# A bidirectional RWKV-7 scan inside a hybrid encoder layer: 32-token blocks laid out by direction and half of the heads, with v's products added in PSUM

## The chip, the cores and the metric

The kernel runs on one core of one Trainium2 chip. A core has a matrix engine (TensorE, in the profile PE for matmuls and PEld for weight loads), a vector engine (VectorE, DVE), a scalar engine (ScalarE, ACT), a general engine (GpSimd, POOL) and a sync engine (SP) whose queue issues most of the DMAs. Each engine takes its instructions in order and waits on semaphores of the others. Matmuls read SBUF and write PSUM, which has eight banks of 512 fp32 columns on 128 partitions; DVE and ACT carry results from PSUM back to SBUF. The metric is the device time of one execution in microseconds (us).

## The reference

The program is one encoder layer for 2048 tokens of width 1024: a normalisation, one wide projection, an RWKV-7 branch that is scanned forwards and backwards, a dilated attention branch, a merge and a mixture of experts. The change touches only the RWKV-7 scan. There are 8 heads of 64 channels, and for each head and direction a state S of 64 x 64:

```python
def step(S, inp):
    r_t, w_t, k_t, v_t, a_t, b_t = inp
    sa = jnp.einsum('bhij,bhj->bhi', S, a_t)
    S = S * w_t[:, :, None, :] + sa[..., None] * b_t[:, :, None, :] + v_t[..., None] * k_t[:, :, None, :]
    return S, jnp.einsum('bhij,bhj->bhi', S, r_t)
...
for d, reverse in enumerate((False, True)):
    ...
    wkv = wkv + wkv7_scan(rh, heads(decay), kd, vh, -kk, kk * ah, reverse)
```

## The kernel before

The scan is done in chunks of 32 tokens (`CH`), 64 steps in all. Step j takes chunk j for the forward direction (d = 0) and chunk 63 - j for the backward one (d = 1), for all 8 heads at once. Inside a chunk the recurrence becomes small matrix products. With A (from the normalised keys) and R (from r) stacked in `ar`, B and K stacked in `bk`, and their transposes in `bt`:

- Z = A S + (A K) v is the right-hand side, 32 x 64 for each head and direction.
- U = inverse x Z, where the inverse is of the triangular 32 x 32 matrix made from A B.
- S' = S + B' U + K' v, after which S is scaled with the chunk's decay `WC`.
- Y = R S + (R B) U + (R K) v is the output, written to `y_d`.

Three kinds of work surround the steps. `prep(i, hh)` prepares 128 tokens (four chunks) for four of the heads: gates by small matmuls (line 431), exponentials, `bk` and `ar` (lines 469 to 474), PE transposes into `bt` (line 479), and the products `bk` x `ar`, masked into `M` (lines 488 and 490). `invert(jj)` inverts the triangular matrices of 256 tokens: DVE transposes them from `M` into `X` (line 513), DVE and POOL eliminate column by column, and DVE transposes back (line 534). `add_v(i, d)` (lines 406 and 412) adds the product of A K and v into the same tile that holds v, ahead of the steps. `dense()` is the other large part: it multiplies the hidden state with the attention and gate columns of the projection, as matmuls of 256 or 512 columns (lines 686 and 690), from weights that come by DMA (line 628) and are split in two parts by ACT and DVE (lines 630 and 631).

The text of the program sets how these are woven: `fill(n)` puts n units of `dense()` (six matmuls of 256 columns or three of 512) behind each part. A step calls it three times through `between` (3.1 units each), `prep` and `invert` at each of their `yield`s. A scheduler then settles the order on each engine, close to that of the text. PE's order is fixed from there on: where a matmul waits, all behind it wait.

In the layout before, a block of 32 tokens of one chunk lies on 32 partitions and all 8 heads lie along the free dimension. Chunks of even number have partitions 0 to 63, those of odd number 64 to 127, and the two directions of a step always have different parity. In the tile `uv` the first 32 partitions of a half take U (and before it the product of A K and v), the other 32 hold v; so one matmul over 64 partitions multiplies U and v together (lines 583 and 591). The matmuls of a step thus use 64 x 64, 64 x 32 (K x M) or 32 x 32 places of the array. U is written back in pieces by DVE (line 574) and ACT (line 576). PSUM banks: `pre` two, `ZY` two, `Up` one, `Sp` one, and two for `dense`.

```python
for ds_, d, c4, b, qc, M in info:
    PE.matmul(ZY[b:b + 64, o], AR[i, h // 4][ds_, h % 4, c4], St[ds_, h], start=h == 0, stop=False, ...)
...
PE.matmul(Up[d][b + h % 2 * 32:b + h % 2 * 32 + 32, h // 2], M[b:b + 32, qc, h, 0:CH], Zs[b:b + 32, o], ...)
```

Of the kernel before, what the change touches and what calls it, by code (L numbers as in the profile page):

```python
# [23 lines left out]
H = 8  # L24
# [18 lines left out]
def hybrid_layer_kernel(ctx, tc, x, positions, norm1_g, w_in, mu_prev, mu_next, w_decay0, w_decay_up, a_gate0,  # L43
# [289 lines left out]

    NC = T // CH
# [16 lines left out]
    nc.sync.dma_start(upw[64:128], a_gate_up[0].rearrange("d p c -> p d c"))  # L351
    msk = mk(sc, [128, 2, 64], F32, "msk")
# [7 lines left out]
    for p in range(1, 4):  # L360
        V.tensor_copy(msk[p * 32:(p + 1) * 32], msk[0:32])
# [21 lines left out]
    AR, BT, UV = {}, {}, {}  # L383
    MR = [mk(sc, [128, 3, 2, H, 64], F32, f"M{d}") for d in range(2)]
    rkk = rkk_d.rearrange("(w a) (e n) t -> n w a e t", w=3, e=2)
    fl = "p a b -> p (a b)"

    def load_v(i):


        uv = UV[i] = mk(sc, [128, 4, HD], F32, "uv", bufs=2)
        vc = v_d.rearrange("(c s) f -> c s f", s=CH)
        for j in range(4 * i, 4 * i + 4):
            for d, c in enumerate((j, NC - 1 - j)):
                p = c % 2 * 64
                nc.sync.dma_start(uv[p + 32:p + 64, j % 4], vc[c])

    def add_v(i, d):

        uv, M = UV[i], MR[d][:, i % 3]  # L400
        pa = mk(psA, [128, 2, H // 2, N], F32, "pre", bufs=2)
        for s in range(4):
            c = s if d == 0 else 3 - s
            for h in range(H):
                p, o = c % 2 * 64, c % 2 * 64 + h % 2 * 32
                PE.matmul(pa[o:o + 32, s // 2, h // 2], M[p + 32:p + 64, c // 2, h, 0:CH],
                          uv[p + 32:p + 64, s, h * N:(h + 1) * N], start=True, stop=True)
        for p in range(2):
            s = p if d == 0 else 1 - p
            for e in range(2):  # L410
                o = p * 64 + e * 32
                S.activation(uv[p * 64:p * 64 + 32, s::2].rearrange("p s (h e n) -> p s h e n", e=2, n=N)[:, :, :, e],
                             pa[o:o + 32], AF.Copy)

    def prep(i, hh):

        ti = (i, NT - 1 - i)
        tk = [slice(t * 128, (t + 1) * 128) for t in ti]
        ld = mk(wk, [128, 3, 4, 128], F32, "ld", bufs=1)
        for d in range(2):  # L420
            for w in range(3):
                nc.sync.dma_start(ld[d * 64:(d + 1) * 64, w].rearrange("n (a e) t -> n a e t", e=2),
                                  rkk[:, w, 2 * hh:2 * hh + 2, :, tk[d]])
        r, k, kk = (ld[:, w] for w in range(3))
        t = [mk(wk, [128, 4, 128], F32, f"t{m}") for m in range(2)]
        for m in range(2):
            z = mk(psA, [128, 4, 128], F32, "pre", bufs=2)
            for h4 in range(4):
                h = hh * 4 + h4
                for d in range(2):  # L430
                    PE.matmul(z[d * 64:(d + 1) * 64, h4], upw[m * 64:(m + 1) * 64, d, h * 64:(h + 1) * 64],
                              sx[m * 64:(m + 1) * 64, tk[d]], start=True, stop=True)
            for h4 in range(4):
                o = 8 * m + hh * 4 + h4
                S.activation(t[m][:, h4], z[:, h4], AF.Tanh, scale=0.5, bias=Q[:, o:o + 1])
            yield
# [11 lines left out]
        hs = slice(hh * 4, hh * 4 + 4)  # L448
        S.activation(WC[0:64, 4 * i:4 * i + 4, hs].rearrange("p c h -> p h c"), cs[0:64, :, CH - 1::CH], AF.Exp)
        for c in range(4):  # L450

            j = 4 * i + 2 - c
            if j >= 0:
                S.activation(WC[64:128, j, hs], cs[64:128, :, c * CH + CH - 1], AF.Exp, scale=-1.0)
        yield
        kf = mk(wk, [128, 4, 128], F32, "cs")
        for h4 in range(4):
            h = hh * 4 + h4
            S.activation(kf[:, h4], ta[:, h4], AF.Identity, scale=Q[:, 24 + h:25 + h], bias=Q[:, 16 + h:17 + h])
# [3 lines left out]
        bt = BT[i, hh] = mk(sc, [128, 2, 4, 128], F32, "bt", bufs=6)  # L463
        bk = mk(wk, [128, 4, 4, 64], F32, "bk")
# [11 lines left out]
        for cp in range(2):  # L476
            pt = mk(psA, [128, 4, 128], F32, "pre", bufs=2)
            for h4 in range(4):
                PE.transpose(pt[:, h4], bk[:, h4, 2 * cp:2 * cp + 2].rearrange("p c x -> p (c x)"), ident)
            S.activation(bt[:, cp], pt, AF.Copy)  # L480
        for d in range(2):
            yield
            pm = mk(psA, [128, 2, 4, 64], F32, "pre", bufs=2)
            for cp in range(2):
                for h4 in range(4):
                    for p in range(2):
                        c = 2 * cp + p
                        PE.matmul(pm[p * 64:(p + 1) * 64, cp, h4], bk[d * 64:(d + 1) * 64, h4, c],
                                  ar[d * 64:(d + 1) * 64, h4, c], start=True, stop=True)
            V.tensor_tensor(MR[d][:, i % 3, :, hs], pm, msk[:, d, None, None, :].to_broadcast([128, 2, 4, 64]),  # L490
                            op=OP.mult)
        yield
        pb = mk(psA, [128, 4, 128], F32, "pre", bufs=2)
        for h4 in range(4):
            PE.matmul(pb[h4 * 32:(h4 + 1) * 32, 0], rkb[:, hh * 4 + h4], kf[:, h4], start=True, stop=True)
        bs = mk(wk, [128, 128], F32, "bs")
        S.activation(bs, pb[:, 0], AF.Copy)
        for d in range(2):
            nc.sync.dma_start(bon_d[d, hs, tk[d]], bs[d:128:32])

    def invert(jj):
# [4 lines left out]
        for d in range(2):  # L506
            M = MR[d][:, lo:hi + 1:hi - lo].rearrange("p i c h x -> p i (c h) x")
            for p in range(2):
                g = (2 * d + p) * 32
                src = M[p * 64:p * 64 + 32, :, :, 0:CH].rearrange("p i q t -> p t i q")  # L510
                xv = X[g:g + 32] if d == 1 else X[g:g + 32].rearrange("p x y -> p y x")
                xv = xv.rearrange("p t (i q) -> p t i q", i=2)
                V.transpose(xv, src)
                views.append((src, xv))
# [24 lines left out]
    def step(j, between):  # L539
        nonlocal St  # L540
        last = j == NC - 1
        i = j // 4
        if j:
            V.tensor_tensor(St, St, WC[:, j - 1, :, None].to_broadcast([128, H, 64]), op=OP.mult)
        ZY = mk(psA, [128, 512], F32, "ZY", bufs=2)
        cc = (j, NC - 1 - j)
        info = []
        for d, c in enumerate(cc):
            info.append((slice(d * 64, d * 64 + 64), d, c % 4, (c % 2) * 64, c // 2 % 2, MR[d][:, i % 3]))
        uv = UV[i][:, j % 4]  # L550
        for h in range(H if j else 0):
            o = slice(h * 64, h * 64 + 64)
            for ds_, d, c4, b, qc, M in info:
                PE.matmul(ZY[b:b + 64, o], AR[i, h // 4][ds_, h % 4, c4], St[ds_, h], start=h == 0, stop=False,
                          skip_group_check=True)
        Zs = mk(wk, [128, 512], F32, "Zs")
        if j:
            V.tensor_tensor(Zs, ZY, uv, op=OP.add)
        else:
            V.tensor_copy(Zs, uv)  # L560
        between(0)


        Up = [mk(psA, [128, H // 2, 64], F32, t) for t in ("Up", "Sp")]
        for h in range(H):
            o = slice(h * 64, h * 64 + 64)
            for ds_, d, c4, b, qc, M in info:
                PE.matmul(Up[d][b + h % 2 * 32:b + h % 2 * 32 + 32, h // 2], M[b:b + 32, qc, h, 0:CH], Zs[b:b + 32, o],
                          start=True, stop=True)
        for ds_, d, c4, b, qc, M in info:  # L570
            uh = uv[b:b + 32].rearrange("p (h e n) -> p h e n", e=2, n=N)
            for e in range(2):
                if d == 0:
                    V.tensor_copy(uh[:, :, e], Up[d][b + e * 32:b + e * 32 + 32])
                else:
                    S.activation(uh[:, :, e], Up[d][b + e * 32:b + e * 32 + 32], AF.Copy)
        between(1)
        if not last:
            Sp = mk(psA, [128, H, 64], F32, "Sp")
            for h in range(H):  # L580
                o = slice(h * 64, h * 64 + 64)
                for ds_, d, c4, b, qc, M in info:
                    PE.matmul(Sp[ds_, h], BT[i, h // 4][b:b + 64, qc, h % 4, ds_], uv[b:b + 64, o], start=True,
                              stop=True)
            Sn = mk(sc, [128, H, 64], F32, "St", bufs=2)
            V.tensor_tensor(Sn, Sp, St, op=OP.add)
            St = Sn
        for h in range(H):
            o = slice(h * 64, h * 64 + 64)
            for ds_, d, c4, b, qc, M in info:  # L590
# [3 lines left out]
        if j:  # L594
            S.activation(Ys, ZY, AF.Copy)
        for ds_, d, c4, b, *_ in info:
            if j == 0:
                S.activation(Ys[b + 32:b + 64], ZY[b + 32:b + 64], AF.Copy)
# [945 lines left out]
```

## Time and profile before

| | |
|---|---|
| runs, median of 3 | 3421.84 us (3415.53 to 3463.06) |
| profiled execution, its own time | 3408.95 us |
| its span, first to last instruction | 3407.2 us |
| PE busy in the span | 3131.7 us (92%) |
| DVE busy | 2340.0 us (69%) |
| ACT busy | 1630.8 us (48%) |
| POOL busy | 607.2 us (18%) |
| stretch of the scan | 424 to 1856 us |

A row of the timeline gives the start, the length, engine, line, operation, the tile written and those read, the shapes and the count of merged instructions, and in square brackets the idle time before it and what ended it. A row by line gives total busy time and the mean of one in ns after the first bar, and the engine's idle time ahead of the group after the second. A row of waits gives the total in us, how often, and the longest. A row by stretch gives its length, then for each engine the busy time and the count of instructions, the granted clock of TensorE as a share of full speed, the busy share of the DMA engines and GB/s. Matmuls overlap, so a group's busy time is less than its count times its mean, and each matmul in fp32 appears as two records of a matmul and two of a weight load.

### The profile page before, as it was taken

Reading aid. Unit: us, or ns where it says so; the run is one execution under the profiler, and the core shown is the slowest. Engines: PE = TensorE matmul, PEld = TensorE weight load, DVE = VectorE, ACT = ScalarE, POOL = GpSimd, SP = SyncE. Lnnn points to the kernel's source line nnn. Section 1 sums busy time; section 2 is a strip of 40 time slices with the busy share of each in tenths; the row PEclk is TensorE's granted clock in tenths of the full one; section 3 lists DMA queues with packets and bytes.
Section 4 is the critical chain, followed back from the end, with each engine's and each line's share of the span. In section 5 each row is a group of like instructions: output and inputs, shape, how many; then the busy total and the mean of one; then the engine's idle time right before and its main releaser. Section 6 shows DMA issues by size and latency. Waiting matters only on the chain. (4 is left out here: it accounts for less than half of the span.)

```text
span 3407.2 us, 72671 instructions
## 1 busy us (share of the span) xinstructions
PE 3131.7 (92%) x29105; PEld 2544.4 (75%) x29105; DVE 2340.0 (69%) x4364; ACT 1630.8 (48%) x3129; POOL 607.2 (18%) x728
## 2 busy tenths in 40 slices
PE   6999989999998989898989998989886999999997
PEld 4888778778876888688867886777775666777775
DVE  7243268677968787769674665667765677888885
ACT  5333344645464535463534765112122566777764
POOL 1000012121212021202020000433422311122231
PEclk8999989999999999998999999999998999999999
DMA  8234233443334323343334554434332799999996
GB/s 303 75 126 144 77 118 108 121 148 115 98 117 147 114 88 115 115 134 97 107 102 137 180 158 150 131 121 140 116 110 103 265 309 305 337 338 338 335 315 208
DMA packets 375953, 567.73 MB, mean 167 GB/s; under 512 B 32462, under 2 KB 232726, under 8 KB 370876
## 3 DMA queue, kind: packets, MB, share of 16 engines
q1 hardware_dynamic: 351100, 497.89, 44.3%
q0 software_dynamic: 13408, 53.10, 5.6%
q10 hardware_dynamic: 11104, 12.06, 1.2%
q8 instruction: 230, 3.77, 0.5%
q14 instruction: 111, 0.91, 0.1%
HBM read 444.05 MB, written 121.64 MB: 166 GB/s over the span
## 5 line engine op out<-in xcount | busy, mean ns | idle before, releaser
L686 PE MATMUL dn<-wh,hk 128*128 128x256 f32 x3456 | 478.0, 297 | 26.2 <-DVE wh L631 17.7
L1237 DVE TENSOR_TENSOR wh<-raw,wh 128x1024 fp32r<-128x1024 f32 x376 | 442.6, 1222 | 77.8 <-ACT wh L1236 77.2
L686 PEld LDWEIGHTS dn<-wh,hk 128*128 128x128 f32 x3456 | 447.4, 201 | 44.6 <-DVE wh L631 20.0
L1236 ACT ACTIVATE wh<-raw 128x1024 fp32r<-128x1024 f32 x384 | 386.9, 1053 | 144.6 <-DMA raw<-in_w_down_dram 60.8
L690 PE MATMUL dn<-hk,wh 128*128 128x512 f32 x1536 | 397.2, 406 | 26.0 <-DVE wh L631 17.0
L1366 PE MATMUL pgu<-wh,xT 128*128 128x512 f32 x1536 | 374.7, 400 | 2.1 <-ACT xT L1341 2.1
L690 PEld LDWEIGHTS dn<-hk,wh 128*128 128x128 f32 x1536 | 281.8, 191 | 101.0 <-DVE wh L631 23.8
L1366 PEld LDWEIGHTS pgu<-wh,xT 128*128 128x128 f32 x1536 | 285.5, 189 | 79.0 <-issue 7.3
L631 DVE TENSOR_TENSOR wh<-raw,wh 128x512 fp32r<-128x512 f32 x272 | 204.1, 754 | 132.7 <-ACT wh L630 131.5
L630 ACT ACTIVATE wh<-raw 128x512 fp32r<-128x512 f32 x272 | 170.7, 631 | 216.1 <-DMA raw<-in_w_in_dram 154.4
L280 PE MATMUL pp<-hq,wh 128*128 128x512 f32 x1008 | 253.8, 409 | 0.0
L280 PEld LDWEIGHTS pp<-hq,wh 128*128 128x128 f32 x1008 | 195.0, 195 | 46.5 <-ACT hq L217 0.4
L1122 PE MATMUL px<-wO,mT 128*128 128x512 f32 x768 | 207.7, 417 | 8.5 <-ACT mT L1112 5.9
L471 POOL TENSOR_TENSOR t<-t,ld 128x512 f32<-128x512 f32 x32 | 52.8, 1651 | 878.6 <-DVE t L460 612.7
L1410 PE MATMUL py<-wh,hT 128*128 128x512 f32 x768 | 191.4, 401 | 0.4 <-ACT hT L1388 0.4
L1122 PEld LDWEIGHTS px<-wO,mT 128*128 128x128 f32 x768 | 145.2, 197 | 46.2 <-ACT mT L1112 8.3
L1410 PEld LDWEIGHTS py<-wh,hT 128*128 128x128 f32 x768 | 140.5, 188 | 33.0 <-issue 1.2
L1302 POOL DMA_INDIRECT out_dram<-ys,IDX x49 | 91.0, 1857 | 315.1 <-issue 107.2
L283 ACT ACTIVATE u<-pp 128x512 f32<-128x512 f32 x56 | 61.2, 1093 | 161.1 <-PE pp L280 123.6
L1106 PE MATMUL ab<-yT,wA 128*128 128x256 f32 x768 | 118.1, 298 | 16.2 <-DVE tg L1108 12.8
L1326 POOL DMA_INDIRECT xg<-h_d,IDX x49 | 74.4, 1518 | 276.1 <-PE tx L1340 173.2
L1106 PEld LDWEIGHTS ab<-yT,wA 128*128 128x128 f32 x768 | 100.0, 192 | 30.6 <-DVE tg L1108 21.1
(421 smaller groups left out, 5770.9 us busy)
## 6 DMA issues: line engine op xcount, KB each, us to landing
raw<-in_w_in_dram SPq DMA_DIRECT2D x286, 256.0 KB
raw<-in_w_gate_dram SPq DMA_DIRECT2D x64, 1024.0 KB
raw<-in_w_up_dram SPq DMA_DIRECT2D x64, 1024.0 KB
raw<-in_w_down_dram SPq DMA_DIRECT2D x64, 1024.0 KB
ld<-rkk_d SPq DMA_DIRECT2D x192, 128.0 KB
g_d<-gs SPq DMA_DIRECT2D x64, 256.0 KB
tg<-g_d SPq DMA_DIRECT2D x128, 128.0 KB
qkr<-qkv_d SPq DMA_DIRECT2D x62, 256.0 KB
```

The source lines that it names most:

```text
L280: PE.matmul(pp, whs[k // 4][:, a, k % 4], hq[q][k // 2][:, k % 2, b], start=n == 0, stop=n == 3 * KT - 1)
L630: S.activation(wh[:, 0], raw, AF.Copy)
L631: V.tensor_tensor(wh[:, 1], raw, wh[:, 0], op=OP.subtract)
L686: PE.matmul(pp[e][:, j * 256:(j + 1) * 256], lhs(2 * e + j, hk, k, a), wk_[:, b], start=k + j + m == 0, stop=k + j + m == KT + 2, skip_gro ...
L690: PE.matmul(pp[e], wk_[:, a, e * 128:e * 128 + 128], hk[k // 2][:, k % 2, b], start=k + m == 0, stop=k + m == KT + 1)
L1106: PE.matmul(pa, wt[k][:, a, cs_], src[:, k, b], start=n == 0, stop=n == 3 * nk - 1)
L1122: PE.matmul(px, mT[:, k, a], wO[k][:, b, fs], start=n == 0, stop=n == 3 * KT - 1)
L1236: S.activation(wh[:, 0, ks], raw[:, ks], AF.Copy)
L1237: eng.tensor_tensor(wh[:, 1, ks], raw[:, ks], wh[:, 0, ks], op=OP.subtract)
L1302: G.indirect_dma_start(out=x2_d, out_offset=bass.IndirectOffsetOnAxis(ap=idx, axis=0), in_=src, in_offset=None, bounds_check=T - 1, oob_is ...
L1366: PE.matmul(pgu[n], xT[:, x_, 4 * a + k], wh[:, w_, k], start=a + k + m == 0, stop=a + k + m == 6)
L1410: PE.matmul(py[f], hT[:, x_, 2 * a + k], wh[:, w_, k, f * 512:(f + 1) * 512], start=a + k + m == 0, stop=a + k + m == 4)
```

## The change

A block is now 32 tokens of one direction d and one half e of the heads: it lies on partitions 64 d + 32 e, and four heads lie along the free dimension. All four blocks of a step (two directions, two halves) fill the 128 partitions whatever the chunk's number. `MB` holds the products with B, `MK` those with K (in the blocks of the other direction, so that rows and columns of the array differ), `VT` holds v alone, and `bt` is split in the same way.

- `add_v` and its evacuations go. The products of A K and R K with v go into the PSUM tiles `ZU` and `Yp` at the start of a step, K' v into `Sp`; the products with the state and with U are added there.
- The product with the state is cut from 64 x 64 pieces to 64 x 32 (A and R apart), those of U and v from K = 64 to K = 32.
- Zs is a copy of 128 x 256 by DVE, U one copy of 128 x 256 by ACT, Ys a copy of 128 x 256.
- The DVE transposes of `invert` are one for each direction on 64 partitions, where there were two on 32.
- In `prep` both gates' matmuls are written into two PSUM tiles in turn, the PE transposes are 16 of 64 partitions, the products `bk` x `ar` are 64 of 64 x 32 in place of 32 of 64 x 64, `bt` is copied in three pieces, and `bk` is written in halves.
- DMAs: v and y_d in pieces of one block, `ld` by direction and one of two heads in place of direction and kind, the bonus by block.
- PSUM banks: `pre` two, `ZU` one, `Yp` one, `Sp` two.

```diff
-    for p in range(1, 4):
-        V.tensor_copy(msk[p * 32:(p + 1) * 32], msk[0:32])
+    V.tensor_copy(msk[32:64], msk[0:32])
+    for d in range(2):
+        V.tensor_copy(msk[64:96, d], msk[0:32, 1 - d])
+        V.tensor_copy(msk[96:128, d], msk[0:32, 1 - d])
...
+    DE4 = [(d, e) for d in range(2) for e in range(2)]
+    def block(d, e):
+        return slice(d * 64 + e * 32, d * 64 + e * 32 + 32)
...
-                nc.sync.dma_start(uv[p + 32:p + 64, j % 4], vc[c])
-    def add_v(i, d):
...
+                for e in range(2):
+                    nc.sync.dma_start(VT[i][block(1 - d, e), j % 4], vc[c, e])
...
-        for cp in range(2):
-            pt = mk(psA, [128, 4, 128], F32, "pre", bufs=2)
-            for h4 in range(4):
-                PE.transpose(pt[:, h4], bk[:, h4, 2 * cp:2 * cp + 2].rearrange("p c x -> p (c x)"), ident)
-            S.activation(bt[:, cp], pt, AF.Copy)
+        pt = [mk(psA, [128, 4, 2, 64], F32, "pre", bufs=2) for _ in range(2)]
+        for s in range(4):
+            for g in range(2):
+                for d in range(2):
+                    ds_, c = slice(d * 64, d * 64 + 64), (s, 3 - s)[d]
+                    PE.transpose(pt[d][:, s, g], bk[ds_, g, c].rearrange("p x e t -> p (x e t)"), ident[ds_, ds_])
+        S.activation(bt[:, 0], pt[0], AF.Copy)
+        for x in range(2):
+            S.activation(bt[64 - x * 64:128 - x * 64, 1], pt[1][x * 64:x * 64 + 64], AF.Copy)
...
+                for x in range(2):
+                    for d, e in DE4:
+                        ds_, c = slice(d * 64, d * 64 + 64), (s, 3 - s)[d]
+                        PE.matmul(pm[x][block(d ^ x, e), s, g], bk[ds_, g, c, x, e],
+                                  ar[ds_, 2 * e + g, c], start=True, stop=True)
...
+            ds_ = slice(d * 64, d * 64 + 64)
+            src = MB[ds_, lo:hi + 1:hi - lo].rearrange("p i s h x -> p i (s h) x")[:, :, :, 0:CH]
...
+            V.transpose(xv, src)
...
+        ZU = mk(psA, [128, 2, 4, 64], F32, "ZU")
+        Yp = mk(psA, [128, 4, 64], F32, "Yp")
+        mb, mkk, v = MB[:, i % 3, s], MK[:, i % 3, s], VT[i][:, s]
+        for h in range(4):
+            o = slice(h * 64, h * 64 + 64)
+            for x, T_ in enumerate((ZU[:, 0], Yp)):
+                for d, e in DE4:
+                    k_ = block(1 - d, e)
+                    product(T_[block(d ^ x, e), h], mkk[k_, h, x * CH:(x + 1) * CH], v[k_, o], h == 0, j == 0 and x == 0)
+        if not last:
+            Sp = mk(psA, [128, 2, 512], F32, "Sp")
...
+                    product(Sp[d * 64:d * 64 + 64, e, o], BT[i, h // 2][k_, d, s, h % 2], v[k_, o], h == 0, False)
+        for h in range(4 if j else 0):
+            for x, T_ in enumerate((ZU[:, 0], Yp)):
+                for d, e in DE4:
+                    ds_ = slice(d * 64, d * 64 + 64)
+                    product(T_[block(d ^ x, e), h], AR[i, h // 2][ds_, 2 * e + h % 2, (s, 3 - s)[d], x * CH:(x + 1) * CH],
+                            St[ds_, 4 * e + h], False, x == 0)
+        Zs = mk(wk, [128, 4, 64], F32, "Zs")
+        V.tensor_copy(Zs, ZU[:, 0])
         between(0)
+                product(ZU[b_, 1, h], mb[b_, h, 0:CH], Zs[b_, h], h == 0, True)
+        U = mk(wk, [128, 4, 64], F32, "U")
+        S.activation(U, ZU[:, 1], AF.Copy)
         between(1)
...
+                    product(Sp[d * 64:d * 64 + 64, e, h * 64:h * 64 + 64], BT[i, h // 2][b_, d, s, h % 2], U[b_, h],
+                            False, True)
...
+                product(Yp[block(1 - d, e), h], mb[b_, h, CH:], U[b_, h], False, True)
+        Ys = mk(wk, [128, 4, 64], F32, "Ys")
+        S.activation(Ys, Yp, AF.Copy)
...
         between(2)
```

Three places in the order of the engines. First PE in the middle of the scan, from the filler ahead of a step to that step's U, before the change (a name is the tile written, then those read; `uv` holds v, `M` the chunk products, `dn` is the filler's bank, and each row's count is in matmuls):

```order
L686 MATMUL dn_17063<-wh_1891_16817,hk_16928 128x256 x12
L406 MATMUL pre_17266<-uv_16871,M_349_2749 32x64 x32
L554 MATMUL ZY_17304<-St_17203,ar_15085 64x64 x8
L554 MATMUL ZY_17304<-St_17203,ar_15579 64x64 x8
L488 MATMUL pre_17323<-ar_17097,bk_17099 64x64 x16
L686 MATMUL dn_17045<-wh_1905_16932,hk_16988 128x256 x12
L686 MATMUL dn_17063<-wh_1905_16932,hk_16988 128x256 x6
L568 MATMUL Up_17360<-Zs_17321,M_349_2749 32x64
L568 MATMUL Sp_17361<-Zs_17321,M_350_2750 32x64
```

The same place of PE's order after it (the rows into ZU and Yp from `uv`, and those from `St`, each come four times in turn):

```order
L693 MATMUL dn_19191<-hk_13530,wh_1799_19075 128x512 x3
L551 MATMUL ZU_19365<-uv_17401,Mk_2752 32x64 x4
L551 MATMUL Yp_19366<-uv_17401,Mk_2752 32x64 x4
...
L551 MATMUL Sp_19399<-uv_17401,bt_16530 64x64 x8
L551 MATMUL Sp_19399<-uv_17401,bt_17205 64x64 x8
L551 MATMUL ZU_19365<-St_19264,ar_16529 32x64 x4
L551 MATMUL Yp_19366<-St_19264,ar_16529 32x64 x4
...
L693 MATMUL dn_19457<-hk_13171,wh_1776_18825 128x512 x6
L551 MATMUL ZU_19365<-Zs_19448,Mb_2751 32x64 x16
```

The products with v stand behind the filler and ahead of those with the state, in tiles of three shapes, and `L406`, which stood there in every second step, is gone.

Second, DVE at the end of an inversion, before (`bk` is the tile `X`):

```order
L530 TENSOR_TENSOR bk_8932<-bk_8932,Zs_8940 128x11
L438 TENSOR_SCALAR t_1088_9486<-t_1088_9486,dirc_2721 128x512
L534 STREAM_TRANSPOSE M_349_2749<-bk_8932 32x32x32 x2
L534 STREAM_TRANSPOSE M_350_2750<-bk_8932 32x32x32 x2
L631 TENSOR_TENSOR wh_1082_9433<-raw_1081_9431,wh_1082_9433 128x512
L558 TENSOR_TENSOR Zs_9477<-ZY_9460,uv_7926 128x512
```

And the end of the same inversion on DVE after the change:

```order
L531 TENSOR_TENSOR bk_10111<-bk_10111,Zs_10117 128x11
L649 TENSOR_TENSOR qs_10320<-qs_10320,ri_10489 128x1024
L535 STREAM_TRANSPOSE Mb_2751<-bk_10111 64x32x32
L650 TENSOR_TENSOR qs_10320<-qs_10320,gq_2761 128x1024
L535 STREAM_TRANSPOSE Mb_2751<-bk_10111 64x32x32
L634 TENSOR_TENSOR wh_1059_10465<-raw_1058_10463,wh_1059_10465 128x512
```

Four transposes have become two, on 64 partitions each, and work on the dense part's `qs` stands between them.

Third, ACT from U of one step to its Ys, before (`uv` is U):

```order
L576 ACTIVATE uv_12391<-Sp_14177 32x4x64 x2
L694 ACTIVATE qs_14023<-dn_14169 128x512
L480 ACTIVATE bt_14148<-pre_14198 128x512
L480 ACTIVATE bt_14148<-pre_14204 128x512
L641 ACTIVATE sq_14401<-qs_14023 128x512
L595 ACTIVATE Ys_14273<-ZY_14121 128x512
```

ACT from U of a step to its Ys after the change, where the most stands between the two:

```order
L581 ACTIVATE U_17558<-ZU_17419 128x256
L434 ACTIVATE wa_17619<-wa_17619 128x512
L437 ACTIVATE wi_17623<-t_1653_17509 128x512
L450 ACTIVATE cs_17732<-t_1654_17510,Q_2705 128x128
L438 ACTIVATE t_1653_17509<-t_1653_17509 128x512
L703 ACTIVATE gs_17573<-dn_17310,drv_77 128x4x128
L450 ACTIVATE cs_17732<-t_1654_17510,Q_2705 128x128 x3
L598 ACTIVATE Ys_17610<-Yp_17420 128x256
```

U and Ys are one piece each, and Ys frees the single bank `Yp`, into which the next step's first matmuls on PE write.

More of the change, by code (lines that the diff above doesn't have):

```diff
@@ new lines, in prep @@
+        yield
+        pm = [mk(psA, [128, 4, 2, 64], F32, "pre", bufs=2) for _ in range(2)]
+        for s in range(4):
+            for g in range(2):
+                for x in range(2):
[3 more added lines that the diff above has]
+                                  ar[ds_, 2 * e + g, c], start=True, stop=True)
+        for x, M in enumerate((MB, MK)):
+            V.tensor_tensor(M[:, i % 3, :, 2 * hh:2 * hh + 2], pm[x],
+                            msk[:, x, None, None, :].to_broadcast([128, 4, 2, 64]), op=OP.mult)
+            yield
@@ L541, in step @@
         last = j == NC - 1
-        i = j // 4
+        i, s = j // 4, j % 4
         if j:
             V.tensor_tensor(St, St, WC[:, j - 1, :, None].to_broadcast([128, H, 64]), op=OP.mult)
[L545 to L551, printed above, removed]
-            o = slice(h * 64, h * 64 + 64)
-            for ds_, d, c4, b, qc, M in info:
-                PE.matmul(ZY[b:b + 64, o], AR[i, h // 4][ds_, h % 4, c4], St[ds_, h], start=h == 0, stop=False,
-                          skip_group_check=True)
@@ new lines, in product @@
+        def product(out, lhsT, rhs, start, stop):
+            PE.matmul(out, lhsT, rhs, start=start, stop=stop, skip_group_check=True)
+        for h in range(4):
+            o = slice(h * 64, h * 64 + 64)
+            for x, T_ in enumerate((ZU[:, 0], Yp)):
[4 more added lines that the diff above has]
+            Sp = mk(psA, [128, 2, 512], F32, "Sp")
+            for h in range(4):
+                o = slice(h * 64, h * 64 + 64)
+                for d, e in DE4:
+                    k_ = block(1 - d, e)
+                    product(Sp[d * 64:d * 64 + 64, e, o], BT[i, h // 2][k_, d, s, h % 2], v[k_, o], h == 0, False)
@@ L577, in step @@
+        U = mk(wk, [128, 4, 64], F32, "U")
+        S.activation(U, ZU[:, 1], AF.Copy)
         between(1)
         if not last:
[L579 to L584, printed above, removed]
+            for h in range(4):
+                for d, e in DE4:
+                    b_ = block(d, e)
+                    product(Sp[d * 64:d * 64 + 64, e, h * 64:h * 64 + 64], BT[i, h // 2][b_, d, s, h % 2], U[b_, h],
+                            False, True)
@@ L585, in step @@
             Sn = mk(sc, [128, H, 64], F32, "St", bufs=2)
-            V.tensor_tensor(Sn, Sp, St, op=OP.add)
+            V.tensor_tensor(Sn.rearrange("p (e h) i -> p e (h i)", e=2), Sp[:, :, 0:256],
+                            St.rearrange("p (e h) i -> p e (h i)", e=2), op=OP.add)
             St = Sn
-        for h in range(H):
-            o = slice(h * 64, h * 64 + 64)
-            for ds_, d, c4, b, qc, M in info:
-                PE.matmul(ZY[b + 32:b + 64, o], M[b:b + 64, qc, h, CH:], uv[b:b + 64, o], start=j + h == 0, stop=True,
-                          skip_group_check=True)
@@ L600, in step @@
+        Ys = mk(wk, [128, 4, 64], F32, "Ys")
+        S.activation(Ys, Yp, AF.Copy)
+        for d, c in enumerate((j, NC - 1 - j)):
+            yv = y_d[d, c * CH:(c + 1) * CH].rearrange("s (e f) -> e s f", e=2)
+            for e in range(2):
+                nc.sync.dma_start(yv[e], Ys[block(1 - d, e)].rearrange("p h i -> p (h i)"))
         between(2)
@@ L729, in hybrid_layer_kernel @@
     mixed([prep(0, 0), prep(0, 1), prep(1, 0), prep(1, 1)], FILL_PREP)
-    for d in range(2):
-        add_v(0, d)
     mixed([invert(0)], FILL_FIRST)
@@ L744, in hybrid_layer_kernel @@
             step(8 * jj + s, between)
-            if s in (1, 2):
-                add_v(2 * jj + 1, s - 1)
-            if s in (5, 6) and more:
-                add_v(i2, s - 5)
             if s % 4 == 3:
```

133 lines of the change are left out of this document (44 added, 89 removed).

## The prediction

> **What bounds it now.** I read the busy time by stretch first. The scan, with the dense projection woven in as filler, runs from 424 to 1856 us; nothing outside it is edited, so only this stage can move.
>
> ```profile
> core 0: us, PE busy (x) PEld busy (x) DVE busy (x) ACT busy (x) POOL busy (x), PEclk, DMA share, GB/s
> 424.00:1856.00 1432.00, 1313.30 (x18657) 1133.80 (x18657) 1070.00 (x2095) 699.05 (x1512) 231.23 (x389) 0.96 0.38 115
> ...
> 1208.90:1264.70 55.80, 46.01 (x396) 44.58 (x396) 53.87 (x127) 18.21 (x40) 16.29 (x38) 0.94 0.34 103
> ...
> sum 391.70, PE 330.53 PEld 287.47 DVE 374.39 ACT 135.57 POOL 124.07; mean PE 41.32 PEld 35.93 DVE 46.80 ACT 16.95 POOL 15.51
> ...
> 1264.70:1377.10 112.40, 107.69 (x1936) 90.88 (x1937) 79.14 (x148) 63.15 (x145) 12.70 (x8) 0.97 0.36 106
> ```
>
> PE is busy 1313 of the 1432 us, DVE 1070. The other rows split the stage. The "sum" row covers the eight inversions (first to last of their DVE transposes): there DVE is full (374 of 392 us). In a stretch of eight scan steps, such as the last row, PE is full (108 of 112 us). So a step is paid in PE time and an inversion in DVE time. The waits of PE in the stage agree:
>
> ```profile
> PE Up L568 <- DVE Zs L558: 26.6, 12, 5.2
> PE dn L686 <- DVE wh L631: 17.7, 9, 4.0
> PE dn L690 <- DVE wh L631: 17.0, 15, 3.0
> ```
>
> **The price of a small matmul.** Bursts of each group, from the timeline (start, length, count); the first row is the busy time of L568 alone in a stretch:
>
> ```profile
> 648.60:649.35 0.75, 0.65 (x32) 0.49 (x32) 1.00 0.00 0
> 643.98 1.42 PE L406 MATMUL pre<-uv,M 32*32 32x64 f32 x64
> 645.32 1.15 PE L554 MATMUL ZY<-St,ar 64*64 64x64 f32 x32
> 652.26 1.40 PE L583 MATMUL Sp<-uv,bt 64*64 64x64 f32 x32 [0.66 <-DVE uv L574]
> 653.59 1.08 PE L591 MATMUL ZY<-uv,M 64*32 64x64 f32 x32
> 657.69 1.91 PE L488 MATMUL pre<-ar,bk 64*64 64x64 f32 x64
> 640.67 1.09 PE L431 MATMUL pre<-xwa,upw 64*64 64x128 f32 x16
> 654.60 1.09 PE L479 MATMUL pre<-ident,bk 128*128 128x128 f32 x8
> 648.67 0.24 PE L568 MATMUL Up<-Zs,M 32*32 32x64 f32 x1
> ...
> 648.69 0.24 PE L568 MATMUL Sp<-Zs,M 32*32 32x64 f32 x1
> 648.75 0.21 PE L568 MATMUL Up<-Zs,M 32*32 32x64 f32 x1
> ```
>
> One fp32 matmul is two records (16 of L554 in a step's code, 32 here). A burst less its last record (0.21 to 0.29 us), over the count less one, is the pace of a record: L568 14 ns, L406 19, L554 30, L591 28, L488 27, L431 55, L479 114. The code says why: L554, L583, L591, L488 and L431 alternate between two places of the array, L568 goes round four. One place thus takes a new record each 56 to 60 ns, and places overlap. The last three rows show it: the first and the fourth record of a burst start 0.02 us apart (7 ns from one to the next), and the fifth, on the first one's place, 0.08 us after it. L406 stays for 16 records on two places and then moves to two others; its 19 instead of 28 ns say that PE runs ahead into the next places before the old ones are through.
>
> A change of tile shape costs extra: the last of L583 started at 652.26 + 1.40 - 0.22 = 653.44, the first of L591 0.15 later where 0.06 would be the pace: 0.09 us a change.
>
> **The change on PE.** Before, a step has 32 records each of L554, L568, L583 and L591, and half of a 64-record L406: 0.96 + 0.45 + 0.96 + 0.90 + 0.61 = 3.88 us. Afterwards it has 256: v into ZU and Yp 64, v into Sp 32, state into ZU and Yp 64, U 32, U into Sp 32, U into Yp 32. The groups of 32 go round four places: 14 ns, 15 with 64 columns (a quarter of 60), together 1.86 us. The two groups of 64 go round eight places. No row has eight; bounds are 14 ns (L568, four) and 7 ns (the start spacing above, also an eighth of 56). I take 10, nearer the low end because of L406's running ahead. That gives 1.28, in all 3.14 us: 0.74 less, over 63 steps -46 us (bounds -14 and -71).
>
> [...] No run here shows eight tiles.
>
> Preparation, 32 calls. The gate products (L431) now go round four places: 32 records at 27 instead of 55 ns, -0.87 us; I count 28 calls (-24), as the first four run where PE already waits. The chunk products become 128 records on eight places instead of 64 on two: 128 x 10 = 1.28 against 64 x 28 = 1.79, -16 us (bounds 0 and -29). The transposes become 16 with 64 rows in place of 8 with 128: if two overlap, 16 x 57, as 8 x 114 now; bounds half (-15 us in all) and double (+29), and I take 0. Tile-shape changes in the PE order of the stage rise from 663 to 760: 97 x 0.09 = +9.
>
> **The change on DVE and ACT.**
>
> ```profile
> L513 DVE STREAM_TRANSPOSE bk<-M 32x1024 f32<-32x1024 f32 x32 | 66.3, 2073 | 0.3
> L534 DVE STREAM_TRANSPOSE M<-bk 32x1024 f32<-32x1024 f32 x32 | 65.2, 2039 | 1.0
> L574 DVE COPY uv<-Up 32x256 f32<-32x256 f32 x128 | 53.6, 419 | 34.5 <-PE Sp L568 31.7
> L558 DVE TENSOR_TENSOR Zs<-ZY,uv 128x512 f32<-128x512 f32 x63 | 43.2, 686 | 43.3 <-PE ZY L554 42.9
> L412 ACT ACTIVATE uv<-pre 32x512 f32<-32x512 f32 x128 | 75.1, 587 | 34.3 <-PE pre L406 32.8
> L576 ACT ACTIVATE uv<-Sp 32x256 f32<-32x256 f32 x128 | 47.9, 374 | 75.3 <-PE Sp L568 67.6 <-DVE rt L108 5.4 <-DVE wh L631 0.7
> L595 ACT ACTIVATE Ys<-ZY 128x512 f32<-128x512 f32 x63 | 37.6, 596 | 94.9 <-PE ZY L591 81.7 <-issue 9.5 <-ACT WC L454 2.0
> L480 ACT ACTIVATE bt<-pre 128x512 f32<-128x512 f32 x64 | 35.3, 596 | 28.4 <-PE pre L479 28.3
> 1256.47 8.21 DVE L534 STREAM_TRANSPOSE M<-bk 32x1024 f32<-32x1024 f32 x4
> 1265.45 0.24 PE L568 MATMUL Up<-Zs,M 32*32 32x64 f32 x1 [4.23 <-DVE Zs L558]
> ```
>
> The inverse's transposes go from 64 on 32 partitions to 32 on 64. Partitions work side by side in the other DVE rows (0.42 us for 32x256, 0.69 for 128x512 go with the length), so one should stay at 2.05 us: -66 us of DVE, 8.2 an inversion; if it grew with the partitions, 0. The last two rows are the end of one inversion: PE, through with its filler, stands 4.23 us until four transposes and Zs (0.69 us) are done. With two, DVE is 8.2 us earlier and that wait ends. Floor: PE's own 331 of 392 us, at most 61 us. I take the 26.6 us of PE waits on Zs, and 8 for the clock, granted at 0.94 there: -35 us (bounds 0 and -61).
>
> In the steps DVE loses L574 (54 us) and a part of L558 (63 x 0.27 = 17). ACT loses L412 (75), half of L576 (U is one piece, 64 at 0.37) and 14 of L595, and gains 22 for bt in three copies. Neither is the bound in a step, so I count nothing for what goes. The 22 us for bt and some 4 us of DVE (bk written in halves, 128 at 0.42 in place of 64 at 0.77) are hidden by the same PE work; without it they cost those 26 us.
>
> **What is added to the queues.**
>
> ```profile
> 1039.76 3.22 SPq L396 DMA_DIRECT2D uv<-v_d  x5
> SPq L628 <- DVE wh L631: 242.8, 120, 10.0
> ACT Ys L595 <- PE ZY L591: 81.7, 34, 5.9
> L459 ACT ACTIVATE cs<-t,Q 128x128 f32<-128x128 f32 x128 | 56.5, 493 | 0.2
> L447 ACT ACTIVATE t<-t 128x512 f32<-128x512 f32 x32 | 20.2, 632 | 0.1
> L700 ACT ACTIVATE gs<-dn,drv 128x512 f32<-128x512 f32 x64 | 75.7, 1182 | 55.3 <-PE dn L690 40.3 <-DMA g_d<-gs 5.5 <-issue 5.1
> 641.69 2.35 PE L690 MATMUL dn<-hk,wh 128*128 128x512 f32 x9
> ```
>
> SP issues 256 more DMAs in the stage (v 128 more, y 128, bonus 64, ld 64 fewer). At 0.64 us (3.22 over five) that is 164 us, in bursts of 16 for v ahead of weight pieces. Mostly such a piece waits for its buffer (the second row), so SP has room: between 0 and 16 bursts x 8 x 0.64 = 82 us, I take +10, a third more of PE's waits for wh. Yp has one buffer where ZY had two, so the next step's products of v stand on PE until ACT has copied Ys, and with them everything queued on PE. Between 0 and the rival below; +10.
>
> **Sum.** -46 - 24 - 16 + 9 - 35 + 10 + 10 = -92 us on the profiled execution's 3408.95 us (span 3407.2): 3317. The three runs have 3415.5 to 3463.1, median 3421.8, 13 above it; I forecast 3320.
>
> **Rivals.** (1) Four wide is the limit: 14 ns everywhere, steps -14, chunk products 0: -44, 3365 us. For it: no stretch of the trace is denser than L568. Against: L406.
> (2) The steps' pace is set by DVE, ACT and SP; PE's gain turns into PE waits and only the inversions gain: -35 + 20, 3394 us. For it: DVE at 75% of the stage. Against: PE's 108 of 112 us.
> (3) The other side: Ys comes late. In the new ACT order eight pieces at the most stand between U and Ys: three of 0.63, four of 0.49 and one of 1.18, 5.0 us. PE offers two fillers of nine matmuls (2.35 us) and 0.9 between: 5.6. If ACT starts late, each step waits on PE: 3 us each make +189, 3506 us; it turns to slower from (68 + 92) / 63 = 2.5 us a step. Against it: ACT now waits 81.7 us for PE ahead of Ys, so ACT is early.
> [...]
>
> **Numbers.** My forecast 0.60 (3265 to 3350), rival 1 0.17, rival 2 0.13, rivals 3 and 4 0.07 and 0.03. The range 3265 to 3400 holds the first three; its low end is 7 ns and a better inversion. Within 2%, about what can be told from no change here, is 3353 to 3490. Faster: 0.95 of the forecast, 0.3 of rival 1: 0.62. Same: 0.03 + 0.12 + 0.12 = 0.27. Slower 0.11 with the rest.
>
> **What would show it.** Bursts into ZU and Yp: 64 records in under 0.9 us at 10 ns, 1.1 at 14. Gate products: 32 records in 1.1 us. Each inversion's DVE transposes two by two at 2.05 us and no PE wait on Zs behind them. Waits of PE on Ys should stay under 20 us in all. I am wrong if PE's busy time in the stage does not fall by some 70 us, or falls and its waits rise as much.

## The result and the profile after

The changed kernel takes 3463.9 us (median of 20 runs, 3440.4 to 3479.4), the one before 3415.7 us (20 runs). The ratio is 1.0139, 95% interval 1.0120 to 1.0159: slower by 48 us, where 92 us less was forecast. Executions of one kernel differ by some 1.5% where the granted clock is lower for a time (the kernel before, measured beside half_y: 3409 to 3423 us at 0.955 to 0.960, but 3472 and 3475 us at 0.940 and 0.938); the ratios in this document leave such runs out.

First the row by stretch of the changed kernel's scan, which now runs from 424 to 1906 us (length, busy time of each engine with its count, granted clock, DMA share, GB/s):

```profile
424.00:1906.00 1482.00, 1278.02 (x27015) 1082.98 (x27010) 947.24 (x1990) 606.59 (x1351) 230.69 (x389) 0.93 0.40 111
```

PE is busy 35 us less than before, DVE 123 us less and ACT 92 us less, and yet the stage is 50 us longer. No engine is busy longer; PE has more idle time, and its clock is 0.93 where it was 0.96. The waits of PE in the stage (total in us, times, longest):

```profile
PE ZU L551 <- DVE Zs L574: 60.3, 25, 4.7
PE Yp L551 <- issue: 24.0, 13, 3.1
PE dn L689 <- DVE wh L634: 21.0, 8, 4.2
PE pre L478 <- DVE bk L464: 19.9, 3, 12.0
PE ZU L551 <- issue: 18.5, 13, 3.0
PE pre L489 <- issue: 14.8, 7, 3.5
PE pre L422 <- issue: 7.5, 4, 2.9
...
PE Yp L551 <- ACT Ys L598: 0.7, 2, 0.5
```

Two things are new. PE waits 60 us for Zs (before: 26.6). And there are rows "issue": PE stands, up to 3.5 us at a time, and waits for no semaphore at all. Before the change the stage had one such row, of 0.5 us in all, at a matmul that does have a semaphore to wait for.

To see where the 50 us are, I dealt out each moment of the scan, from the first gate product to the last filler matmul, by PE's records in order of start. What an instruction adds past the end of those before it counts as its own; a stretch in which none runs counts as a wait when the next one waits for a semaphore, and as a pause when it doesn't:

| scan, us | filler | small matmuls | waits | pauses | sum |
|---|---|---|---|---|---|
| before | 839.7 | 473.4 | 116.8 | 0 | 1430 |
| after | 873.1 | 406.3 | 131.1 | 70.7 | 1481 |
| difference | +33.4 | -67.1 | +14.3 | +70.7 | +51 |

The small matmuls brought 67 us, near the 77 forecast for all of PE's terms. It was lost three times over: in pauses, in waits, and in the filler, whose count is the same (3360 matmuls of 256 columns and 1536 of 512) but whose time is 33 us more.

**The pauses.** A stretch of PE's timeline, step by step (start, length, line, tile written and read, merged count, and in brackets the idle time before):

```profile
645.92 0.69 PE L551 MATMUL Sp<-uv,bt 32*64 32x64 f32 x32
...
647.33 2.33 PE L693 MATMUL dn<-hk,wh 128*128 128x512 f32 x9
651.93 0.65 PE L551 MATMUL ZU<-Zs,Mb 32*32 32x64 f32 x32 [2.27 <-DVE Zs L574]
652.51 3.57 PE L693 MATMUL dn<-hk,wh 128*128 128x512 f32 x9
...
660.41 1.48 PE L489 MATMUL pre<-ar,bk 64*32 64x64 f32 x128
661.82 0.26 PE L551 MATMUL ZU<-uv,Mk 32*32 32x64 f32 x4
...
663.48 0.25 PE L551 MATMUL ZU<-uv,Mk 32*32 32x64 f32 x4 [1.31 <-issue]
...
668.95 0.26 PE L551 MATMUL Yp<-St,ar 64*32 64x64 f32 x4 [3.10 <-issue]
```

The burst of v into ZU and Yp is cut in two at 663.48 and that of the state at 668.95, each inside the burst. What stands there is the supply of instructions. The DMA queue that carries code, first in the page of before, then in that of after (packets, MB, share):

```profile
q8 instruction: 230, 3.77, 0.5%
```
```profile
q8 instruction: 295, 4.83, 0.6%
```

Each packet has 16,384 bytes, 16 KB. PE has 58,643 instructions before and 75,355 after (loads, matmuls and a few for semaphores): 255 to a packet in both. With the distances of 254 and 256 in the first reading below, I take a packet for a block of 256 PE instructions. Four readings of the trace tie the pauses to it:

- Counted in PE's loads and matmuls, the pauses at 663.48 and 668.95 are 254 instructions apart, and the next neighbours 256 (696.82 and 700.55), 256 (835.99 and 841.49) and 256 (978.23 and 984.17).
- All 35 pauses of over 0.5 us lie in one narrow band of the block, which moves slowly from place 150 to place 78 over the stage, as the semaphore instructions, which I don't count, add up.
- Each ends 2.2 to 3.4 us after the start of a code packet.
- The shortest spacing of code packets is 3.2 to 3.5 us in before, after, twice_v and half_y (before 3.49, after 3.34). Under 5 us apart are 15 pairs before and 90 after.

So PE gets 256 instructions in some 3.4 us at best, 13 ns each (between the two pauses shown above the packets start 4.9 us apart). A record of a small fp32 matmul is a load and a matmul: 27 ns by supply. Before the change the bursts on four places ran at 14 ns, and the account above has no pauses there; that such bursts, of 32 records, were short enough to live on what was in store is my reading and was not shown. At 10 ns, 128 records use up a block in 1.3 us, and in a step with chunk products some 290 records stand in a row.

**The clock.** In the timeline above nine filler matmuls take 2.33 us, and the same nine 3.57 us behind a wait of 2.27 us. Of 997 filler matmuls that start within 5 us behind an idle time of over 1 us, 508 come at over 1.6 times their spacing, most at nearly double (427 in place of 227 ns for 512 columns); of the other 3644, 108. Before, the scan had 35 idle times of over 1 us, with 241 such slow matmuls behind them; now it has 78. All slow ones together cost 45 us before and 77 us after beyond the full-clock spacing, which is nearly the 33 us of the filler. The trace's own record of the granted clock has two values, 1.0 and 0.5. In the scan it stands at half for 123 us before, in 21 stretches, and for 222 us after, in 47, and each of these stretches has an idle time of over 1 us less than 5 us ahead of it. Of the 99 us more, 79 are stretches that follow pauses alone. Ahead of 33 of the 47 stretches the longest of these idle times is under 3 us.

**The wait for Zs.** DVE around the wait at 651.93:

```profile
647.91 0.43 DVE L451 TENSOR_SCALAR t<-t 128x512 f32<-128x512 f32 x1 [1.61 <-ACT cs L450]
648.25 0.68 DVE L452 TENSOR_TENSOR cs<-cs,ld 128x512 f32<-128x512 f32 x1
650.11 0.42 DVE L468 TENSOR_TENSOR bk<-t,wi 128x256 f32<-128x256 f32 x1 [1.17 <-POOL t L466]
650.46 0.75 DVE L464 TENSOR_TENSOR bk<-cs,wi 128x256 f32<-128x256 f32 x2
651.12 0.42 DVE L468 TENSOR_TENSOR bk<-t,wi 128x256 f32<-128x256 f32 x1
651.46 0.42 DVE L574 COPY Zs<-ZU 128x256 f32<-128x256 f32 x1
```

ZU was complete at about 647.4. The copy starts 4.1 us later, because in DVE's order the preparation of the next tokens stands ahead of it, and that waits for ACT and for POOL while DVE idles. Over all steps the copy starts 1.46 us (median) behind the last product that it needs; before, L558 started 0.12 us behind. PE reaches the place sooner, the preparation does not.

### The profile page after: what moved, and what is told of

Same layout as the page of the kernel before. It is cut to its first block, busy times and chain, and to the rows that moved or that the text cites. A ratio compares the mean times of both kernels' runs of the same rounds, so it can differ in the third digit from the quotient of the medians.

```text
span 3459.6 us, 89389 instructions
## 1 busy us (share of the span) xinstructions
PE 3092.0 (89%) x37489; PEld 2491.9 (72%) x37489; DVE 2219.1 (64%) x4270; ACT 1537.7 (44%) x2968; POOL 611.6 (18%) x728
## 5 line engine op out<-in xcount | busy, mean ns | idle before, releaser
L689 PE MATMUL dn<-wh,hk 128*128 128x256 f32 x3456 | 491.2, 303 | 31.6 <-DVE wh L634 21.0
L689 PEld LDWEIGHTS dn<-wh,hk 128*128 128x128 f32 x3456 | 462.8, 208 | 49.5 <-DVE wh L634 22.5
L693 PE MATMUL dn<-hk,wh 128*128 128x512 f32 x1536 | 410.5, 419 | 10.4 <-DVE wh L634 4.9
L693 PEld LDWEIGHTS dn<-hk,wh 128*128 128x128 f32 x1536 | 293.6, 198 | 87.9 <-DVE wh L634 8.7
L1299 POOL DMA_INDIRECT out_dram<-ys,IDX x49 | 103.4, 2110 | 309.8 <-issue 133.2
L703 ACT ACTIVATE gs<-dn,drv 128x512 f32<-128x512 f32 x64 | 75.8, 1184 | 109.9 <-PE dn L693 83.9
```

The lines of the kernel that those rows point to most:

```text
L689: PE.matmul(pp[e][:, j * 256:(j + 1) * 256], lhs(2 * e + j, hk, k, a), wk_[:, b], start=k + j + m == 0, stop=k + j + m == KT + 2, skip_gro ...
L693: PE.matmul(pp[e], wk_[:, a, e * 128:e * 128 + 128], hk[k // 2][:, k % 2, b], start=k + m == 0, stop=k + m == KT + 1)
L1299: G.indirect_dma_start(out=x2_d, out_offset=bass.IndirectOffsetOnAxis(ap=idx, axis=0), in_=src, in_offset=None, bounds_check=T - 1, oob_is ...
```

## The experiments

Each kernel is the changed one with the edit shown, unless said otherwise. The table has the same account as above for each; the ratio is to the kernel before. The ratio is of the whole program over several runs, the other columns are of the scan alone in one profiled execution, so the two need not move together.

| kernel | ratio (95% interval) | filler | small | waits | pauses | scan |
|---|---|---|---|---|---|---|
| after | 1.0139 (1.0120 to 1.0159) | 873.1 | 406.3 | 131.1 | 70.7 | 1481 |
| even | 1.0118 (1.0092 to 1.0144) | 899.7 | 421.9 | 139.6 | 10.0 | 1471 |
| twice_v | 1.0303 (1.0197 to 1.0409) | 870.2 | 459.5 | 104.6 | 119.5 | 1554 |
| half_y | 0.9903 (0.9873 to 0.9934) | 854.8 | 370.1 | 134.5 | 21.7 | 1381 |
| zs_act | 1.0045 (1.0008 to 1.0081) | 854.2 | 409.0 | 110.2 | 64.1 | 1438 |
| inv4_again | 1.0294 (1.0257 to 1.0330) | 862.3 | 412.1 | 170.0 | 62.0 | 1506 |
| before_z | 0.9971 (0.9952 to 0.9990) | 830.8 | 453.9 | 127.1 | 0 | 1412 |
| q192z | 1.0110 (1.0053 to 1.0166) | 864.5 | 412.7 | 134.7 | 15.5 | 1427 |
| p3 | 0.9997 (0.9977 to 1.0016) | 862.1 | 411.2 | 112.9 | 31.4 | 1418 |

**The same instructions, spread out (even).**

```diff
+    def paid(n):
+        if even[0]:
+            fill(n / 75)
...
             for x, T_ in enumerate((ZU[:, 0], Yp)):
                 for d, e in DE4:
                     product(...)
+            paid(32)
...
             def between(n):
                 next(side, None)
-                fill(FILL_STEP[n] if more else FILL_LAST)
+                if not more:
+                    fill(FILL_LAST)
```

> The changed kernel with the same instructions, but the dense filler dealt out in proportion to the small matmuls (one unit per 75 of their instructions) in place of 3.1 units at three places of a step. Theory code supply (PE's instructions come in blocks of 256, a new one each 3.4 us at the most): the pauses of PE without a releaser, 71 us in the scan, fall below 25 us. Rival (the pauses come from the array or PSUM in the bursts themselves): they stay at 60 to 80 us. Changes between dense and small matmuls double from 463 to 1011, at some 0.1 us each +50 us, so that the time itself moves between -40 and +10 us against the changed kernel.

The rows of PE's waits in the spread kernel that answer to the pauses:

```profile
PE ZU L560 <- issue: 4.5, 4, 1.5
PE pre L496 <- issue: 3.8, 5, 1.4
PE Yp L560 <- issue: 0.7, 2, 0.4
```

The code is as long (295 packets), the bursts are shorter, and the pauses fall from 71 to 10 us. The matmuls, their places of the array and their PSUM banks are the same, so these alone do not make the pauses; that the pauses lie on the borders of code blocks points to the supply. The time fell by some 7 us only, less than the two intervals tell apart: the filler cost 27 us more and the small matmuls 16 us more, as PE changes between the two 1011 times in place of 463. The clock is not what the filler lost by here: it stood at half for 147 us of this scan, in place of 222.

**More and less code (twice_v, half_y).** In twice_v the first loop of a step runs `for h in (0, 1, 2, 3) * 2`. In half_y the products of v and of the state skip `Yp`:

```diff
-            for x, T_ in enumerate((ZU[:, 0], Yp)):
+            for x, T_ in enumerate((ZU[:, 0],)):
```

> The changed kernel with the products of v into ZU and Yp done twice in each step (the second time over the first): 64 more records of 10 ns a step. Theory pace: +0.64 us a step, +41 us, pauses without a releaser stay near 71 us. Theory code supply: 128 more instructions a step at 3.4 us per 256 are 1.7 us, so up to +109 us; about +75 if half of the steps have no slack, and the pauses rise above 100 us.

> The changed kernel that leaves out R S and (R K) v of Y (the products of v and of the state into Yp), so that its output is not the reference's: 64 of a step's 256 records go, 128 of their PE instructions. Theory pace alone: -41 us of PE time (64 steps x 64 x 10 ns), pauses without a releaser stay near 71 us, 3464 becomes about 3423. Theory code supply: the pauses fall to 15 to 40 us as well, and the dense matmuls regain 10 to 20 us of clock: 3345 to 3395. Rival (DVE paces the steps and PE's time is off the path): waits for Zs rise by 30 us or more and the time stays above 3425.

The code packets are 327 and 263, and PE's waits show the pauses, first of twice_v, then of half_y:

```profile
PE ZU L551 <- issue: 48.8, 32, 4.0
...
PE Sp L551 <- issue: 29.5, 14, 4.4
PE Yp L551 <- issue: 22.0, 15, 3.4
```
```profile
PE pre L489 <- issue: 12.4, 5, 3.9
PE ZU L551 <- issue: 4.4, 5, 1.7
```

In half_y, R S and (R K) v are left out of Y, so it shows a cost and is no kernel to use. 64 records a step more lengthen the scan by 73 us, of which the small matmuls themselves are 53 and the pauses 49 (the waits for Zs fall by 30, since PE arrives later). 64 records fewer, worth 36 us of PE, shorten it by 100: 49 us of pauses and 18 us of filler go with them, and the clock stands at half for 157 us in place of 222. The four runs of twice_v took 3532 to 3561 us, and its ratio has a wide interval; the account of the scan is the better measure of it. The count of instructions has a price beyond that of their time, in both directions.

**Zs by another engine (zs_act).**

```diff
-        V.tensor_copy(Zs, ZU[:, 0])
+        S.activation(Zs, ZU[:, 0], AF.Copy)
```

> The changed kernel with the copy Zs made by ACT in place of DVE. Theory DVE queue (Zs stands behind preparation work in DVE's order, which waits for POOL and ACT): PE's waits for Zs fall from 60 to under 25 us, and the time by 30 to 60 us against the changed kernel, since the clock recovers too. Rival (the chain through the step is itself too long, or ACT is as late as DVE): the waits stay between 45 and 80 us and the time within 15 us.

```profile
PE ZU L551 <- ACT Zs L574: 6.5, 4, 2.9
```

That is what is left of the 60.3 us. The gain is 32 us (1.0139 less 1.0045, of 3416). The wait was DVE's queue, not the chain through the step. All waits together fell by 21 us only, as PE now waits longer for ACT's copies of U and `bt` (28 us in place of 5). The filler regains 19 us with the idle times. The scan is 43 us shorter; the attention stage, which the edit does not touch, was 20 us longer in the profiled execution (more on it below).

**The inversion's transposes (inv4, inv4_again).**

```diff
-        for d in range(2):
-            ds_ = slice(d * 64, d * 64 + 64)
+        for d, e in DE4:
+            ds_ = block(d, e)
```

> The changed kernel with the inversion's DVE transposes in pieces of 32 partitions again, 64 in place of 32. By the forecast's term they are worth 35 us: 3464 becomes about 3499. Rival (the filler and the order of the inversions hide most of it; PE's idle time in the eight inversions fell by 16 us only): +5 to +20 us.

> The same kernel as inv4 (the changed kernel with the inversion's DVE transposes in pieces of 32 partitions), since its four runs gave 3474 to 3532. Theory DVE queue (DVE's 66 us of transposes are paid nearly in full, as DVE is what PE waits for at Zs and in the inversions): ratio to before 1.027 to 1.033, 45 to 65 us above the changed kernel. Forecast's term: +35 us, ratio 1.024. Rival (hidden): ratio 1.014 to 1.019.

Four runs of inv4 gave 1.0164 (1.0034 to 1.0295), which decides nothing. Six more of the same kernel gave 1.0294. The transposes by line and form, of the changed kernel and of this one:

```profile
L514 DVE STREAM_TRANSPOSE bk<-Mb 64x1024 f32<-64x1024 f32 x16 | 34.1, 2129 | 0.1
L535 DVE STREAM_TRANSPOSE Mb<-bk 64x1024 f32<-64x1024 f32 x16 | 34.0, 2122 | 0.7
```
```profile
L514 DVE STREAM_TRANSPOSE bk<-Mb 32x1024 f32<-32x1024 f32 x32 | 67.6, 2113 | 0.4
L535 DVE STREAM_TRANSPOSE Mb<-bk 32x1024 f32<-32x1024 f32 x32 | 66.9, 2091 | 1.3
```

66 us of DVE come back, and the ratio rises by 53 us (0.0155 of 3416). That does not show that DVE's time is paid nearly in full: in the profiled execution the scan, where all the transposes are, is 25 us longer than in the changed kernel, and the attention stage behind it 21 us longer, at a granted clock of 0.90 where it was 0.99. The scan's 25 us lie between the rival's 5 to 20 and the 35 of the forecast. That the edit brings the lower clock in the attention stage about is not shown.

**One part alone, on the kernel before (before_z).** Its edit, to the kernel before:

```diff
-        for m in range(2):
-            z = mk(psA, [128, 4, 128], F32, "pre", bufs=2)
-            for h4 in range(4):
-                h = hh * 4 + h4
+        z = [mk(psA, [128, 4, 128], F32, "pre", bufs=2) for _ in range(2)]
+        for h4 in range(4):
+            h = hh * 4 + h4
+            for m in range(2):
                 for d in range(2):
-                    PE.matmul(z[d * 64:(d + 1) * 64, h4], ...)
+                    PE.matmul(z[m][d * 64:(d + 1) * 64, h4], ...)
```

> The kernel before with one part of the change alone: the gate products of both gates written into two PSUM tiles in turn, so that they go round four places of the array. Theory PE pace: each call's 32 records fall from 55 to 27 ns, -0.87 us in 28 calls, -24 us, ratio 0.993. Rival (the steps are paced by the chain through DVE, ACT and POOL, and PE's gain becomes waiting): within 5 us, ratio 0.999 to 1.001. The other rival (both gates' ACT work then waits for the whole burst): up to +10 us, ratio 1.003.

Ten us faster (3 to 16 by the interval), between the theory's 24 and the rival's none. In the scan the small matmuls fell by 19.5 us as they should and the filler by 9, and the waits rose by 10, half of what PE gained; the stages behind the scan took 6 us more in the profiled execution. It is the one kernel here that does all of the work and beats the one before, by 0.3%.

**Both mends together (q192z, p3).** Both have Zs on ACT. In q192z the filler is dealt out as in even, but only once 192 instructions of small matmuls have gathered; in p3 it keeps its three places and gets two more:

```diff
-FILL_PREP, FILL_FIRST, FILL_STEP, FILL_INV, FILL_LAST = 4, 6.5, (3.1, 3.1, 3.1), 6.5, 2.5
+FILL_PREP, FILL_FIRST, FILL_STEP, FILL_INV, FILL_LAST = 4, 6.5, (2.5, 2.3, 1.2), 6.5, 2.5
...
                         PE.matmul(pm[x][block(d ^ x, e), s, g], ...)
+            if s == 1 and scanning:
+                fill(1.8)
...
+        if scanning and j < NC - 8:
+            fill(2.4)
         if not last:
             Sp = mk(psA, [128, 2, 512], F32, "Sp")
```

> The changed kernel with two edits: Zs copied by ACT (as in zs_act), and the filler dealt out after each 192 instructions of small matmuls or more (2.6 units at a time) in place of three places of a step. Theory code supply: the pauses without a releaser fall from 64 us (zs_act) to 15 to 35 us, the dense matmuls regain part of their clock, and 200 more changes between dense and small matmuls cost some 16 us; 3432 becomes 3385 to 3415, ratio to before 0.991 to 1.000. Rival (the filler is then missing between Zs, U and their users, and what is saved in pauses comes back as waits): ratio 1.002 to 1.008.

> The changed kernel with Zs copied by ACT and a part of the filler moved into the two longest runs of small matmuls: 1.8 units in the middle of the chunk products, 2.4 behind the products of v into ZU and Yp, for which the three old places give 2.5, 2.3 and 1.2. Theory code supply: pauses without a releaser 64 us (zs_act) to 20 to 40 us, waits for Zs and U under 25 us in all since filler stays there, scan ends 15 to 35 us ahead of zs_act's 1865: 3400 to 3420, ratio to before 0.995 to 1.002. Rival (given back as waits and as changes between dense and small): ratio 1.003 to 1.010.

The waits of p3 that are left at these places:

```profile
PE Yp L554 <- ACT Ys L603: 20.8, 20, 2.6
...
PE Sp L554 <- ACT U L586: 18.0, 7, 4.3
PE pre L490 <- issue: 12.2, 7, 3.1
PE Yp L554 <- issue: 9.8, 9, 2.4
PE ZU L554 <- issue: 7.6, 7, 2.8
```

The pauses are 31 us, the waits for Zs under 7, and new ones for Ys and U have come, since ACT now does more and PE is earlier still. The scan is 12 us shorter than before the change, and the time is the same: 0.9997. In q192z the scan is 54 us shorter than in the changed kernel, but the time only by some 10: its ratio of 1.0110 lies above both of its forecasts. The rest went in the attention stage, which nothing here edits: with the same matmuls it took 289 us there at a granted clock of 0.86, 284 at 0.86 in p3, 275 at 0.90 in zs_act, but 255 at 0.99 in the changed kernel and 259 at 0.98 before:

```profile
1859.00:2148.00 289.00, 281.58 (x1834) 229.32 (x1834) 159.16 (x232) 169.25 (x545) 4.25 (x2) 0.86 0.47 145
```
```profile
1909.00:2164.00 255.00, 243.94 (x1834) 201.40 (x1834) 160.23 (x233) 168.39 (x546) 4.26 (x2) 0.99 0.55 166
```

In all of these traces the stage begins with an idle time of some 5 us and a half clock behind it, but in the changed kernel that half clock lasts 7 us, and in q192z 78 us with PE busy throughout. But for that of inv4, each kernel has one profiled execution here, so whether this goes with the kernel or with the execution is not known. Why the clock stays at half was not tried; it stays open.

## Why the prediction was wrong, step by step

- **The steps on PE, eight places.** The pace was right, the term was not. Bursts on eight places run at 10.0 to 10.2 ns a record (median of 49 whole bursts of the state 10.2, of 23 of the chunk products 10.0), where 10 was taken; four places stay at 14 to 15. Rival 1, 14 ns everywhere, falls. But in the account above, the groups of the steps (with `add_v` before) fell from 292 to 273 us only, 20 where 46 were forecast: each group takes 0.1 to 0.2 us beyond its count times its pace, and a step has six groups now where it had four and, in every second one, a fifth. All PE terms together were -77 us (-46 - 24 - 16 + 9); that the small matmuls fell by 67, so near to it, is partly luck, as the transposes, taken as 0, brought 12 us.
- **The gate products.** 27 ns at best, as forecast, but in 16 of 23 whole bursts of the steps 42 ns and more, up to 53; the 42 was not followed up. They fell by 20 us of the 24 all the same. The transposes, taken as 0, run at 33 ns a record, 0.4 us less a call.
- **What was not in the sum: the added instructions.** The step that failed is that a burst was priced by its pace alone. The change adds 4320 matmuls and transposes, 16,768 loads and matmuls on PE (a transpose is one record, not two), and I let them cost nothing but array time. They cost 71 us of pauses, and with those most of the 33 us of half clock (79 of the 99 us more at half clock follow pauses alone). The profile of before had the row that would have bounded it: 230 code packets, for 256 instructions each, and its trace has some of them 3.5 us apart. At that rate v, state and chunk products of one step alone (576 instructions and more) take 7.7 us of supply, and I gave them 3.
- **Zs.** Forecast: 26.6 us of PE waits on Zs go with the shorter inversion. Measured: 60.5. Those behind inversions fell from 18 to 13 us; those in the middle of the steps rose from 8 to 48. "Neither is the bound in a step" was the failing step: DVE's busy time had room, its order had not. Rival 2 (3394 us, chance 0.13), PE's gain turned into waits for other engines, came nearest to this, but it has no pauses and no half clock in it and still forecast a gain.
- **The inversion's transposes.** Mechanism right: DVE's share fell by 63 us as forecast (66). The size is not settled: undoing it costs 25 us in the scan, where 35 was taken, and 53 us by the ratios, of which a part lies in the attention stage.
- **SP's DMAs, +10.** Not seen: PE's waits for `wh` fell from 35 to 26 us. **Yp's single bank, +10, and rival 3.** Not seen: 0.7 us in all; it appears, 21 us, only in p3, where PE is earlier.
- **The test in the forecast** held: it was to be wrong if PE's busy time fell and its waits rose as much. PE's busy time fell by 35 us and not by some 70, and its idle time rose by 85.

In one line: -67 of small matmuls, +71 of pauses, +33 of half clock, +14 of waits, in which +34 on Zs stand against -20 elsewhere.

## What to carry to other kernels

Price small matmuls by count as well as by time: compare the instructions of the densest stretch with the spacing of the code packets in the trace, and make fewer of them, or spread them, before making them faster; spreading alone gave most of its gain back here in changes between filler and small matmuls (42 us of 61). When one engine gets faster inside an order that is fixed, read what stands ahead of each hand-over in the queues of the others, since busy time says nothing of it. An idle time of over a microsecond on TensorE was often paid twice here, the second time in the matmuls behind it (508 of 997 ran slow). And an edit to one stage is read from that stage: the time of the whole also holds what the clock did in the others (0.86 to 0.99 in the attention stage).

## What the runs showed of the hardware

- Code came in packets of 16 KB, one for each 255 of PE's instructions (230 before, 295 after), never less than 3.2 us apart in before, after, twice_v and half_y; in the changed kernel bursts of small matmuls stood up to 3.5 us at the borders of these blocks without waiting for a semaphore.
- Records of small fp32 matmuls of 64 columns started 10 ns apart on eight places of the array (after), 14 to 15 on four (before and after), 27 to 30 on two (before).
- In the changed kernel's scan 508 of the 997 filler matmuls within 5 us behind an idle time of over 1 us ran slow, and all 47 stretches at half clock (222 us) have such an idle time ahead, the longest under 3 us for 33 of them.
- The clock granted to unchanged code (the attention stage) was between 0.86 and 0.99 in the executions given above, worth up to 34 us; its cause is open.
